# The mLSTM mixer of layer 1: scores and sums of values as three rounded passes on split operands, and the o gate kept in the place of y

## The chip, the cores and the metric

One core of a Trainium2 chip runs the whole program. The metric is the device time of one execution in microseconds. The kernel before took 2152.68 us (median of three runs, 2150.7 to 2155.58).

PE is the matmul engine (TensorE), PEld its weight loads, DVE the vector engine, ACT the scalar engine, POOL GpSimd, SP the engine that issues most DMAs. Each engine works through its instructions in order and waits on semaphores for the others.

## The reference

A backbone of four layers over 256 latent tokens and 256 context tokens of width 2048. Layer 1 is a bidirectional mLSTM with 8 heads (128 wide for q and k, 256 wide for v). The part that matters here, for one chunk of one direction:

```python
q, k, v, o, g, z = jnp.split(h @ w_in, idx, axis=-1)
...
s = jnp.einsum('bhtd,bhsd->bhts', q, k) * jnp.exp(dmat - m_t[..., None])
num = a[..., None] * jnp.einsum('bhtd,bhde->bhte', q, C) + jnp.einsum('bhts,bhse->bhte', s, v)
h = num / jnp.maximum(jnp.abs(den), jnp.exp(-m_t))[..., None]
...
y = jax.nn.sigmoid(o.astype(f32)).reshape(B, T, M_HEADS, M_DV) * h
y = _rmsnorm(y, hn.reshape(M_HEADS, M_DV)).reshape(B, T, M_V).astype(z.dtype)
return (y * jax.nn.silu(z)) @ w_out
```

The forward and backward directions are added. All is float32.

## The kernel before

All 512 tokens are worked on together, context first. Every big projection is a `gemm` (line 240): 16 contraction blocks of 128, four PSUM banks, and three rounded passes for each product. The weights are cast to `wh` (rounded, float32r) on ACT (L256), the remainder `wl` is taken on DVE (L257), the activations stand as `h` and `l` in the same way, and L298 adds `h*wh + h*wl + l*wh`. One such projection has 192 passes of 512 columns. `wh` and `wl` have three buffers each, the raw weights four.

Layer 1 has four pairs of heads. For each pair four projections run after each other: q and k (`done_qk`), v (`done_v`), o (`done_o`), z (`done_z`). Each has its `done` function called for each of its four banks, as soon as that bank is complete; the next projection takes the same four banks again (`psA`), so it waits for whatever `done` reads from them.

Between the projection's matmuls the mixer's own work of the pair is woven in, by a hand-written order of PE: a generator `core` is moved on by a step each time enough credit has come together (`fill.give`, a rate for each step of the projection; `CORE1` is the rate for the core during the o and z projections). One step of the projection is six matmuls. The core goes over eight tiles (two heads, four blocks of 128 queries each), each in three stages:

- `stage_a`: scores, one full-precision matmul of q against 256 keys (blocks 0 and 1, context) or 512 keys (blocks 2 and 3) into a bank `xb` (L803); the decay factors on ACT (`ef`, `eb`); products, row sums and the normalisation on DVE (L817 to L832). The result is `big`.
- `stage_b`: `big` is transposed on PE (L839) and copied to `wt` by ACT (L841).
- `stage_c`: the sums of values, full-precision matmuls of `wt` against `v` over two or four key blocks, 256 columns each (L848), then the o gate.

The four banks of `psX` (`xb`) go round among these. PE's order is written out by hand; for DVE, ACT and the other engines a scheduler orders the instructions when the program is built.

The o gate of `tanh` of o's projection is one tile `to` of 128 x 4 x 512. Tiles whose sums are ready before o is complete are copied to `yp` (L852) and gated later; the others are gated from the bank (L906). L908 then squares for the norm, into a scrap tile `jk`. `finish` (called `fin` in the weave) normalises, transposes on PE (L889), multiplies with hn and the z gate `zs` (L890) and stores the result to DRAM (L934), or splits it for the last pair.

In the background, other layers' modulation vectors are computed on DVE (`ada_dve`, L217): multiply and sum over 128 x 1024 tiles that come by DMA, moved on at the rates `BR1`. Below they are called multiplies. They stand in DVE's queue among all the rest.

The gates of all heads (`gates`) are computed once, during pair 0's v projection, in two scratch tiles, `sa` in the place of `yp` and `sb` in the place of `zs`.

Of the kernel before, what the change touches and what calls it, by code (L numbers as in the profile page):

```python
# [23 lines left out]

DV0 = (2, 4, 6)

NPE1, CORE1, ATT = 4, 0.4, 1.2
MIX3, MIX0, MIX1, FR0, BR0, AR0 = 0.55, 0.9, 0.7, 0.8, 0.34, 0.17

BR1 = ((0, 0.35, 0.25, 0.25), (0.35, 0.35, 0.25, 0.25), (0.4, 0.4, 0.3, 0.3), (0.5, 0.5, 0.35, 0.35))  # L30
# [21 lines left out]
def _build(tc, nc, top, A, out):  # L52
    V, S, G, T, Q = nc.vector, nc.scalar, nc.gpsimd, nc.tensor, nc.sync
# [644 lines left out]
    with ExitStack() as st:  # L698
        p1 = pool(st, "l1", reuse_waits="tile")

        def w2(name):
            return p1.tile([P, 512], F32, tag="w2", name=name, bufs=5)

        bgate = p1.tile([P, 1], F32, name="bgate")
        Q.dma_start(bgate, A["bgate"])
# [3 lines left out]
        def gates():  # L709


            gw = wp.tile([P, 2, 512], F32, tag="raw", name="gw", bufs=WRAW)
            Q.dma_start(gw[:, 0, :], A["w1gate"])
            Q.dma_start(gw[:, 1, :128], A["gsum"])

            pq = bank()
            for k4 in range(4):
                for ip in range(2):
                    for q in range(4):
                        kt = 4 * k4 + q  # L720
                        T.matmul(pq[32 * q:32 * q + 32, :], gw[:, 0, 32 * kt:32 * kt + 32], hl[kt][ip].bitcast(F32),
                                 start=k4 + ip == 0, stop=k4 == 3 and ip == 1)
                yield
            sq = w2("gq")
            S.copy(sq, pq)
            yield
            yield
            pg = bank()
            T.matmul(pg, gw[:, 1, :128], sq, start=True, stop=True)
            sa = pY.tile([P, 4, 512], F32, tag="yp", name="sa", bufs=1)  # L730
            sb = pY.tile([P, 4, 512], F32, tag="zs", name="sb", bufs=1)
            ri, rl, rb, rM, z0 = sa[:, 0, :], sa[:, 1, :], sa[:, 2, :], sa[:, 3, :], sb[:, 0, :]
# [25 lines left out]
            for n, src in enumerate((ri, rM, rb)):  # L758
                r = sb[:, n + 1, :]
# [21 lines left out]
        def core(c):  # L781
# [16 lines left out]
            def stage_a(hh, i, ub, um):  # L798
# [4 lines left out]
                T.matmul(sp[:, :ns], c.qk[:, hh, dg], c.qk[:, 2 + hh, :ns], start=True, stop=True)  # L803
# [31 lines left out]
            def stage_b(hh, i, big):  # L835
                ns = 256 if i < 2 else 512
                pt = bank()
                for k in range(ns // 128):
                    T.transpose(pt[:, 128 * k:128 * k + 128], big[:, 128 * k:128 * k + 128], ident)  # L839
                wt = p1.tile([P, 512], F32, tag="wt", name="wt", bufs=2)  # L840
                S.copy(wt[:, :ns], pt[:, :ns])  # L841
                return wt

            def stage_c(hh, i, wt):
                nb = 2 if i < 2 else 4
                po = bank()
                for k in range(nb):
                    T.matmul(po[:, :256], wt[:, 128 * k:128 * k + 128], c.v[:, k, 256 * hh:256 * hh + 256],  # L848
                             start=k == 0, stop=k == nb - 1)
                ys = c.yp[:, i, 256 * hh:256 * hh + 256]  # L850
                if c.pend is not None:
                    S.copy(ys, po[:, :256])  # L852
                    c.pend.append((hh, i))
                else:
                    c.gate(hh, i, po[:, :256])

            tiles = [(hh, i) for hh in range(2) for i in range(4)]
            u = {0: load(0)}
            w = {0: stage_a(0, 0, *u[0])}
            yield  # L860
            for n, (hh, i) in enumerate(tiles):
                if n == 2:
                    u[1] = load(1)
                if n + 1 < 8:
                    h2, i2 = tiles[n + 1]
                    w[n + 1] = stage_a(h2, i2, *u[h2])
                    yield
                if n:
                    stage_c(*tiles[n - 1], wt)
                    yield  # L870
                wt = stage_b(hh, i, w[n])
                yield
            yield
            stage_c(*tiles[-1], wt)
            yield

        def finish(c, sink):
            S.activation(c.ssq, c.ssq, AF.Sqrt, bias=eps4, scale=1.0 / 256)
# [16 lines left out]
        def make_pair(p):  # L895
            c = Pair()
            c.p = p
            c.qk = p1.tile([P, 4, 512], F32, tag="qk", name="qk", bufs=1)
            c.v = p1.tile([P, 4, 512], F32, tag="v", name="v", bufs=1)
            c.to = p1.tile([P, 4, 512], F32, tag="to", name="to", bufs=1)  # L900
            c.ssq = pY.tile([P, 8], F32, tag="ssq", name="ssq", bufs=2)
            c.pend = []

            def gate(hh, i, src):
                ys = c.yp[:, i, 256 * hh:256 * hh + 256]
                V.scalar_tensor_tensor(ys, c.to[:, i, 256 * hh:256 * hh + 256], 1.0, src, ALU.add, ALU.mult)  # L906
                jk = p1.tile([P, 256], F32, tag="jk", name="jk", bufs=1)
                S.activation(jk, ys, AF.Square, accum_out=c.ssq[:, 4 * hh + i:4 * hh + i + 1])  # L908

            c.gate = gate  # L910

            def done_qk(b, ps):
                S.activation(c.qk[:, b, :], ps, AF.Copy, scale=128 ** -0.5 if b < 2 else 1.0)

            def done_v(b, ps):
                S.copy(c.v[:, b, :], ps)

            def done_o(b, ps):
                S.activation(c.to[:, b, :], ps, AF.Tanh, scale=0.5)
                if b == 3:  # L920
                    pend, c.pend = c.pend, None
                    for hh, i in pend:
                        gate(hh, i, c.yp[:, i, 256 * hh:256 * hh + 256])

            def done_z(b, ps):
                tz = w2("tz")
                S.activation(tz, ps, AF.Tanh, scale=0.5)
                V.scalar_tensor_tensor(c.zs[:, b, :], tz, 1.0, ps, ALU.add, ALU.mult)

            c.done = (done_qk, done_v, done_o, done_z)  # L930
            return c

# [17 lines left out]
        for p in range(4):  # L950
# [9 lines left out]
            c.zs = pY.tile([P, 4, 512], F32, tag="zs", name="zs", bufs=1)  # L960
# [410 lines left out]
```

## Time and profile before

| | |
|---|---|
| median of three runs | 2152.68 us |
| the profiled execution | 2155.34 us, of which 2153.5 us are its span |
| granted TensorE clock, mean | 0.987 |
| HBM traffic | 435.9 MB read, 13.7 MB written |

In the 40 slices of the page each is 53.8 us, and layer 1 lies in slices 11 to 24:

```
PE   6899999999999999999999999999999999999998
DVE  4867888856787787799666678765645665567666
ACT  4332242223333324232332343223336544545444
PEclk7999999999999999999999999999999999999999
```

Each digit is the busy share in tenths. A row of the profile's groups gives line, engine, operation, tiles and shapes, then busy time, mean duration of one, and the idle time of that engine just before the group with what ended it. A float32 matmul stands as two records. Durations of matmuls overlap; the distance of two starts tells what one costs.

### The profile page before, as it was taken

To read this page: it belongs to the slowest core of one execution; us is meant where nothing else is said; L and a number is where in the kernel's file an instruction comes from. 1 tells how busy PE (TensorE), PEld (TensorE's weight loads), DVE (VectorE), ACT (ScalarE), POOL (GpSimd) and SP (SyncE) were. 2 spreads that over 40 slices of the span, in tenths; PEclk is the share of its full clock that TensorE was granted. 3 is DMA by queue.
4 is the path that set the end of the run, shared out by engine and by line. 5 is a ranking of instruction groups with operands and counts; after the bars stand their busy time and mean duration, and the time that the engine had idled before them with its cause. 6 is when DMAs were issued, how large, how long until landed. Compare 5 with 4: busy or idle time off the path is not lost. (4 is left out here: it accounts for less than half of the span.)

```text
span 2153.5 us, 29391 instructions
## 1 busy us (share of the span) xinstructions
PE 2091.3 (97%) x11190; PEld 1725.9 (80%) x11190; DVE 1527.3 (71%) x2793; ACT 812.2 (38%) x1338; POOL 19.3 (1%) x29
## 2 busy tenths in 40 slices
PE   6899999999999999999999999999999999999998
PEld 2668777788788888888888888888787777999986
DVE  4867888856787787799666678765645665567666
ACT  4332242223333324232332343223336544545444
POOL 0000000000000000000000000000000000000000
PEclk7999999999999999999999999999999999999999
DMA  9775778872465565477668667983243454564464
GB/s 349 275 265 191 250 276 282 322 271 95 153 209 166 199 224 179 162 250 254 202 207 305 226 235 280 335 312 107 88 137 124 141 176 138 173 195 138 153 194 147
DMA packets 126127, 451.52 MB, mean 210 GB/s; under 512 B 14224, under 2 KB 16784, under 8 KB 123296
## 3 DMA queue, kind: packets, MB, share of 16 engines
q1 hardware_dynamic: 125696, 448.71, 61.0%
q8 instruction: 88, 1.44, 0.3%
q10 hardware_dynamic: 288, 0.92, 0.1%
q14 instruction: 55, 0.45, 0.1%
HBM read 435.91 MB, written 13.66 MB: 209 GB/s over the span
## 5 line engine op out<-in xcount | busy, mean ns | idle before, releaser
L257 DVE TENSOR_TENSOR wl<-wraw,wh 128x1024 fp32r<-128x1024 f32 x400 | 489.1, 1224 | 404.6 <-ACT wh L256 393.4
L298 PE MATMUL acc<-h,wh 128*128 128x512 f32 (+1 forms) x1936 | 689.3, 356 | 6.1 <-ACT h L395 3.9
L256 ACT CAST wh<-wraw 128x1024 fp32r<-128x1024 f32 x400 | 419.1, 1049 | 724.4 <-PE acc L298 581.4
L298 PE MATMUL acc<-l,wh 128*128 128x512 f32 (+1 forms) x1936 | 671.7, 347 | 3.0 <-DVE l L396 1.8
L298 PE MATMUL acc<-h,wl 128*128 128x512 f32 (+1 forms) x1936 | 670.4, 346 | 1.3 <-DVE wl L257 1.1
L298 PE MATMUL acc<-wh,h 128*128 128x512 f32 x1024 | 427.0, 417 | 3.5 <-DVE xn L1019 2.2
L298 PEld LDWEIGHTS acc<-h,wh 128*128 128x128 f32 x1936 | 367.8, 190 | 61.9 <-issue 11.2
L298 PEld LDWEIGHTS acc<-l,wh 128*128 128x128 f32 x1936 | 367.3, 190 | 51.2 <-DVE l L396 3.5
L298 PEld LDWEIGHTS acc<-h,wl 128*128 128x128 f32 x1936 | 367.9, 190 | 45.7 <-DVE wl L257 2.3
L298 PE MATMUL acc<-wh,l 128*128 128x512 f32 x1024 | 401.2, 392 | 0.5 <-DVE l L396 0.5
L298 PE MATMUL acc<-wl,h 128*128 128x512 f32 x1024 | 399.7, 390 | 0.0
L217 DVE SCALAR_TENSOR_TENSOR araw<-araw,cb 128x1024 f32<-128x1024 f32 x300 | 364.7, 1223 | 12.0 <-DMA araw<-in_ada_t_dram 9.8
L298 PEld LDWEIGHTS acc<-wh,h 128*128 128x128 f32 x1024 | 192.8, 188 | 52.0 <-issue 14.5
L298 PEld LDWEIGHTS acc<-wl,h 128*128 128x128 f32 x1024 | 193.0, 188 | 44.6 <-issue 8.4
L298 PEld LDWEIGHTS acc<-wh,l 128*128 128x128 f32 x1024 | 192.5, 188 | 42.8 <-DVE l L396 1.3
L217 DVE SCALAR_TENSOR_TENSOR ajunk<-araw,cb 128x1024 f32<-128x1024 f32 x172 | 209.8, 1220 | 0.0
L187 PE MATMUL xb<-araw,cpad 128*32 128x256 f32 x672 | 56.7, 439 | 15.4 <-DMA araw<-in_ada_p_dram 12.7
L187 PEld LDWEIGHTS xb<-araw,cpad 128*32 128x32 f32 x672 | 17.6, 116 | 44.9 <-DMA araw<-in_ada_p_dram 26.9
L395 ACT ACTIVATE h<-mu,ada 128x256 fp32r<-128x256 f32 x80 | 36.9, 502 | 35.9 <-DVE mu L394 35.9
L848 PE MATMUL xb<-v,wt 128*128 128x256 f32 x192 | 46.7, 379 | 0.0
L453 ACT ACTIVATE sq<-rn 128x256 f32<-128x256 f32 (+1 forms) x48 | 24.7, 515 | 56.1 <-DVE rn L447 54.3
L908 ACT ACTIVATE jk<-yp 128x256 f32<-128x256 f32 x32 | 13.3, 417 | 78.8 <-DVE yp L906 78.8
(223 smaller groups left out, 1480.3 us busy)
## 6 DMA issues: line engine op xcount, KB each, us to landing
araw<-in_ada_t_dram SPq DMA_DIRECT2D x300, 512.0 KB, 5.2
wraw<-in_w1in_dram SPq DMA_DIRECT2D x128, 512.0 KB, 4.4
araw<-in_ada_p_dram SPq DMA_DIRECT2D x84, 512.0 KB, 5.4
wraw<-in_w2in_dram SPq DMA_DIRECT2D x80, 512.0 KB, 3.5
wraw<-in_w0g_dram SPq DMA_DIRECT2D x32, 512.0 KB, 5.5
wraw<-in_w0o_dram SPq DMA_DIRECT2D x32, 512.0 KB, 5.7
wraw<-in_w1o_dram SPq DMA_DIRECT2D x32, 512.0 KB, 7.0
wraw<-in_w2o_dram SPq DMA_DIRECT2D x32, 512.0 KB, 4.2
```

What stands on the lines that cost most here:

```text
L187: T.matmul(ps[32 * q:32 * q + 32, :256], cpad[:, 4 * kq + q, :], rv[:, q, :], start=kq == 0, stop=kq == 3)
L217: V.scalar_tensor_tensor(o, rv, 1.0, cb[:, v + 2 - nv, part], ALU.mult, ALU.mult, accum_out=am[:, v, i, hf:hf + 1])
L256: S.copy(wh, raw)
L257: pace.append(V.tensor_tensor(wl, raw, wh.bitcast(F32), ALU.subtract).ins)
L298: T.matmul(o, lhsT, rhs, start=start, stop=stop)
L395: S.activation(h[:, c], u, AF.Identity, bias=ada[:, l, SH, s, kt:kt + 1])
L453: S.activation(sq[:, c], rn[:, b, c], AF.Square)
L848: T.matmul(po[:, :256], wt[:, 128 * k:128 * k + 128], c.v[:, k, 256 * hh:256 * hh + 256], start=k == 0, stop=k == nb - 1)
L908: S.activation(jk, ys, AF.Square, accum_out=c.ssq[:, 4 * hh + i:4 * hh + i + 1])
```

## The change

Scores and sums of values become three passes of float32r operands, in the way of the projections.

- `c.qk` and `c.v` are now rounded (float32r). `done_qk` and `done_v` also write the remainders `ql` and `vl` on DVE, from the PSUM bank. `stage_b` rounds `wt` and writes its remainder `wtl` on DVE.
- L804: scores as `q*k + q*kl + ql*k`. L852: sums as `wt*v + wt*vl + wtl*v`.
- The tile `to` is no longer held: `done_o` writes `tanh` into `yp`, where the result will come (L937), or, where a tile's sum already stands there, into a small tile of 256 columns (L934), and gates it at once. The squares go into the PSUM bank that was just read; `jk` is gone.
- `ql` takes the place of `zs` in `pY` while the core runs. So `fin` of the pair before must be through when the first bank of q arrives, and the core must be through when the first bank of z arrives.
- `sb` becomes four tiles `w2`, which has six buffers rather than five.
- The core's order: two tiles' scores ahead, then for each tile b, the scores of the tile after next, c. `CORE1` goes from 0.4 to 0.56.

```diff
-NPE1, CORE1, ATT = 4, 0.4, 1.2
+NPE1, CORE1, ATT = 4, 0.56, 1.2
...
-            return p1.tile([P, 512], F32, tag="w2", name=name, bufs=5)
+            return p1.tile([P, 512], F32, tag="w2", name=name, bufs=6)
...
-            sb = pY.tile([P, 4, 512], F32, tag="zs", name="sb", bufs=1)
+            sb = [w2(f"sb{n}") for n in range(4)]
...
-                T.matmul(sp[:, :ns], c.qk[:, hh, dg], c.qk[:, 2 + hh, :ns], start=True, stop=True)
+                for ip, (q, k) in enumerate(((c.qk, c.qk), (c.qk, c.ql), (c.ql, c.qk))):
+                    T.matmul(sp[:, :ns], q[:, hh, dg], k[:, 2 + hh, :ns], start=ip == 0, stop=ip == 2)
...
-                wt = p1.tile([P, 512], F32, tag="wt", name="wt", bufs=2)
+                wt = p1.tile([P, 512], F32R, tag="wt", name="wt", bufs=2)
+                wtl = p1.tile([P, 512], F32R, tag="wtl", name="wtl", bufs=2)
                 S.copy(wt[:, :ns], pt[:, :ns])
-                return wt
+                V.tensor_tensor(wtl[:, :ns], pt[:, :ns], wt[:, :ns].bitcast(F32), ALU.subtract)
+                return wt, wtl
...
                 for k in range(nb):
-                    T.matmul(po[:, :256], wt[:, 128 * k:128 * k + 128], c.v[:, k, 256 * hh:256 * hh + 256],
-                             start=k == 0, stop=k == nb - 1)
+                    for ip, (w, v) in enumerate(((wt[0], c.v), (wt[0], c.vl), (wt[1], c.v))):
+                        T.matmul(po[:, :256], w[:, 128 * k:128 * k + 128], v[:, k, 256 * hh:256 * hh + 256],
+                                 start=k + ip == 0, stop=k == nb - 1 and ip == 2)
                 ys = c.yp[:, i, 256 * hh:256 * hh + 256]
-                if c.pend is not None:
+                if (hh, i) in c.to:
+                    c.gate(hh, i, ys, po[:, :256])
+                else:
                     S.copy(ys, po[:, :256])
-                    c.pend.append((hh, i))
-                else:
-                    c.gate(hh, i, po[:, :256])
+                    c.po.add((hh, i))
...
             for n, (hh, i) in enumerate(tiles):
-                if n == 2:
+                if n == 1:
                     u[1] = load(1)
-                if n + 1 < 8:
-                    h2, i2 = tiles[n + 1]
-                    w[n + 1] = stage_a(h2, i2, *u[h2])
-                    yield
-                if n:
-                    stage_c(*tiles[n - 1], wt)
-                    yield
-                wt = stage_b(hh, i, w[n])
+                wt = stage_b(hh, i, w.pop(n))
                 yield
-            yield
-            stage_c(*tiles[-1], wt)
-            yield
+                if n + 2 < 8:
+                    h2, i2 = tiles[n + 2]
+                    w[n + 2] = stage_a(h2, i2, *u[h2])
+                yield
+                stage_c(hh, i, wt)
+                yield
...
-            def gate(hh, i, src):
+            def gate(hh, i, to, src, junk=None):
                 ys = c.yp[:, i, 256 * hh:256 * hh + 256]
-                V.scalar_tensor_tensor(ys, c.to[:, i, 256 * hh:256 * hh + 256], 1.0, src, ALU.add, ALU.mult)
-                jk = p1.tile([P, 256], F32, tag="jk", name="jk", bufs=1)
-                S.activation(jk, ys, AF.Square, accum_out=c.ssq[:, 4 * hh + i:4 * hh + i + 1])
+                V.scalar_tensor_tensor(ys, to, 1.0, src, ALU.add, ALU.mult)
+                S.activation(src if junk is None else junk, ys, AF.Square, accum_out=c.ssq[:, 4 * hh + i:4 * hh + i + 1])
...
             def done_qk(b, ps):
-                S.activation(c.qk[:, b, :], ps, AF.Copy, scale=128 ** -0.5 if b < 2 else 1.0)
+                if b == 0:
+
+                    fill.finish(f"fin{p - 1}")
+                    c.ql = pY.tile([P, 4, 512], F32R, tag="zs", name="ql", bufs=1)
+                sc = 128 ** -0.5 if b < 2 else 1.0
+                S.activation(c.qk[:, b, :], ps, AF.Copy, scale=sc)
+                V.scalar_tensor_tensor(c.ql[:, b, :], ps, sc, c.qk[:, b, :].bitcast(F32), ALU.mult, ALU.subtract)

             def done_v(b, ps):
                 S.copy(c.v[:, b, :], ps)
+                V.tensor_tensor(c.vl[:, b, :], ps, c.v[:, b, :].bitcast(F32), ALU.subtract)

             def done_o(b, ps):
-                S.activation(c.to[:, b, :], ps, AF.Tanh, scale=0.5)
-                if b == 3:
-                    pend, c.pend = c.pend, None
-                    for hh, i in pend:
-                        gate(hh, i, c.yp[:, i, 256 * hh:256 * hh + 256])
+                for hh in range(2):
+                    cols = slice(256 * hh, 256 * hh + 256)
+                    ys = c.yp[:, b, cols]
+                    if (hh, b) in c.po:
+                        to = p1.tile([P, 256], F32, tag="to", name="to", bufs=1)
+                        S.activation(to, ps[:, cols], AF.Tanh, scale=0.5)
+                        gate(hh, b, to, ys, ps[:, cols])
+                    else:
+                        S.activation(ys, ps[:, cols], AF.Tanh, scale=0.5)
+                        c.to.add((hh, b))

             def done_z(b, ps):
+                if b == 0:
+                    fill.finish(f"core{p}")
+                    c.zs = pY.tile([P, 4, 512], F32, tag="zs", name="zs", bufs=1)
                 tz = w2("tz")
```

How this moves instructions is shown at three places, by rows of the two built programs (line, operation, what is written and read, shape).

First PE in pair 0, at a tile with four key blocks. Before, a tile's transposes (L839), the scores of a later tile (L803) and the sums (L848) stand apart, with passes of the projection between them; here the sums with the passes on either side:

```order
L298 MATMUL acc<-wl,h_4712 128x512
L298 MATMUL acc<-wh,l_4713 128x512
L848 MATMUL xb<-v,wt 128x256 x4
L298 MATMUL acc<-wh,h_4682 128x512
L298 MATMUL acc<-wl,h_4682 128x512
L298 MATMUL acc<-wh,l_4683 128x512
```

The change has, for a tile of four blocks of the same pair, twelve instructions there, each group of three ending with the one that reads `wtl`:

```order
L298 MATMUL acc<-wh,l_4637 128x512
L852 MATMUL xb<-v,wt 128x256
L852 MATMUL xb<-vl,wt 128x256
L852 MATMUL xb<-v,wtl 128x256
L852 MATMUL xb<-v,wt 128x256
L852 MATMUL xb<-vl,wt 128x256
L852 MATMUL xb<-v,wtl 128x256
```

Six of the twelve are shown; the same three follow twice more. A score is one instruction before and three now.

Second DVE in pair 0, at the scores of its last tile (128x512). Before, the remaining steps of that tile follow with little between, and the next two gates:

```order
L817 SCALAR_TENSOR_TENSOR ef,dn<-xb,ef 128x512
L819 SCALAR_TENSOR_TENSOR eb,dn<-xb,eb 128x512
L257 TENSOR_TENSOR wl<-wraw,wh 128x1024
L822 SCALAR_TENSOR_TENSOR da<-dn 128x2
L823 TENSOR_TENSOR da<-da,em 128x2
L824 RECIPROCAL da<-da 128x2
L831 TENSOR_SCALAR ef<-ef,da 128x512
L832 SCALAR_TENSOR_TENSOR ef<-eb,da,ef 128x512
L906 SCALAR_TENSOR_TENSOR yp<-to,xb 128x256
```

In the change, behind the first product of that tile (L818, 128x512), up to the remainder `wtl` of the tile before it:

```order
L820 SCALAR_TENSOR_TENSOR eb,dn<-xb,eb 128x512
L217 SCALAR_TENSOR_TENSOR araw,am<-araw,cb 128x1024
L823 SCALAR_TENSOR_TENSOR da<-dn 128x2
L257 TENSOR_TENSOR wl<-wraw,wh 128x1024
L824 TENSOR_TENSOR da<-da,em 128x2
L910 SCALAR_TENSOR_TENSOR yp<-yp,xb 128x256
L825 RECIPROCAL da<-da 128x2
L217 SCALAR_TENSOR_TENSOR ajunk,am<-araw,cb 128x1024
L832 TENSOR_SCALAR ef<-ef,da 128x512
L217 SCALAR_TENSOR_TENSOR araw,am<-araw,cb 128x1024
L833 SCALAR_TENSOR_TENSOR ef<-eb,da,ef 128x512
L844 TENSOR_TENSOR wtl<-xb,wt 128x512
```

Three multiplies of the background now stand among this tile's steps, and `wtl` (L844), which PE needs, stands behind them. On PE, from the scores of the last tile to the third pass of the sums of the tile before it, there are 40 passes of the projection, the sums of a tile with two blocks, four transposes and two passes.

Third ACT at the last bank of pair 0's o projection. Before, one tanh over the whole bank (the L919 row; the rows around it serve the tiles and the weights):

```order
L256 CAST wh<-wraw 128x1024
L813 ACTIVATE eb<-ub_5424,negM 128x128
L919 ACTIVATE to<-acc 128x512
L256 CAST wh<-wraw 128x1024
L908 ACTIVATE jk,ssq<-yp 128x256
```

In the change, at the same bank: for its first half a tanh (L934), a square into the bank (L911, which needs the gate on DVE between), and then the tanh of the other half (L937):

```order
L934 ACTIVATE to<-acc 128x256
L256 CAST wh<-wraw 128x1024
L911 ACTIVATE acc,ssq<-yp 128x256
L937 ACTIVATE yp<-acc 128x256
L911 ACTIVATE xb,ssq<-yp 128x256
L843 CAST wt<-xb 128x256
```

The bank is free only after the last of its three reads and writes, where before it was free after one.

More of the change, by code (lines that the diff above doesn't have):

```diff
@@ L730, in gates @@
             sa = pY.tile([P, 4, 512], F32, tag="yp", name="sa", bufs=1)
-            sb = pY.tile([P, 4, 512], F32, tag="zs", name="sb", bufs=1)
-            ri, rl, rb, rM, z0 = sa[:, 0, :], sa[:, 1, :], sa[:, 2, :], sa[:, 3, :], sb[:, 0, :]
+            sb = [w2(f"sb{n}") for n in range(4)]
+            ri, rl, rb, rM, z0 = sa[:, 0, :], sa[:, 1, :], sa[:, 2, :], sa[:, 3, :], sb[0]
             S.activation(ri[0:64, :], pg[0:64, :], AF.Identity, bias=bgate[0:64])
@@ L758, in gates @@
             for n, src in enumerate((ri, rM, rb)):
-                r = sb[:, n + 1, :]
+                r = sb[n + 1]
                 V.tensor_copy(r[0:32, :], src[0:32, :])
@@ L847, in stage_c @@
                 for k in range(nb):
-                    T.matmul(po[:, :256], wt[:, 128 * k:128 * k + 128], c.v[:, k, 256 * hh:256 * hh + 256],
-                             start=k == 0, stop=k == nb - 1)
+                    for ip, (w, v) in enumerate(((wt[0], c.v), (wt[0], c.vl), (wt[1], c.v))):
+                        T.matmul(po[:, :256], w[:, 128 * k:128 * k + 128], v[:, k, 256 * hh:256 * hh + 256],
+                                 start=k + ip == 0, stop=k == nb - 1 and ip == 2)
                 ys = c.yp[:, i, 256 * hh:256 * hh + 256]
-                if c.pend is not None:
+                if (hh, i) in c.to:
+                    c.gate(hh, i, ys, po[:, :256])
+                else:
                     S.copy(ys, po[:, :256])
-                    c.pend.append((hh, i))
-                else:
-                    c.gate(hh, i, po[:, :256])
+                    c.po.add((hh, i))
             tiles = [(hh, i) for hh in range(2) for i in range(4)]
             u = {0: load(0)}
-            w = {0: stage_a(0, 0, *u[0])}
+            w = {}
+            for n in range(2):
+                w[n] = stage_a(*tiles[n], *u[0])
+                yield
             yield
             for n, (hh, i) in enumerate(tiles):
-                if n == 2:
+                if n == 1:
                     u[1] = load(1)
-                if n + 1 < 8:
-                    h2, i2 = tiles[n + 1]
-                    w[n + 1] = stage_a(h2, i2, *u[h2])
-                    yield
-                if n:
-                    stage_c(*tiles[n - 1], wt)
-                    yield
-                wt = stage_b(hh, i, w[n])
-                yield
-            yield
-            stage_c(*tiles[-1], wt)
-            yield
+                wt = stage_b(hh, i, w.pop(n))
+                yield
+                if n + 2 < 8:
[3 more added lines that the diff above has]
+                stage_c(hh, i, wt)
+                yield
         def finish(c, sink):
@@ L897, in make_pair @@
             c.p = p
-            c.qk = p1.tile([P, 4, 512], F32, tag="qk", name="qk", bufs=1)
-            c.v = p1.tile([P, 4, 512], F32, tag="v", name="v", bufs=1)
-            c.to = p1.tile([P, 4, 512], F32, tag="to", name="to", bufs=1)
+            c.qk = p1.tile([P, 4, 512], F32R, tag="qk", name="qk", bufs=1)
+            c.v = p1.tile([P, 4, 512], F32R, tag="v", name="v", bufs=1)
+            c.vl = p1.tile([P, 4, 512], F32R, tag="vl", name="vl", bufs=1)
             c.ssq = pY.tile([P, 8], F32, tag="ssq", name="ssq", bufs=2)
-            c.pend = []
@@ L904, in gate @@
-            def gate(hh, i, src):
+            c.to, c.po = set(), set()
+            def gate(hh, i, to, src, junk=None):
                 ys = c.yp[:, i, 256 * hh:256 * hh + 256]
-                V.scalar_tensor_tensor(ys, c.to[:, i, 256 * hh:256 * hh + 256], 1.0, src, ALU.add, ALU.mult)
-                jk = p1.tile([P, 256], F32, tag="jk", name="jk", bufs=1)
-                S.activation(jk, ys, AF.Square, accum_out=c.ssq[:, 4 * hh + i:4 * hh + i + 1])
+                V.scalar_tensor_tensor(ys, to, 1.0, src, ALU.add, ALU.mult)
+                S.activation(src if junk is None else junk, ys, AF.Square, accum_out=c.ssq[:, 4 * hh + i:4 * hh + i + 1])
@@ L959, in _build @@
                 fill.finish(f"fin{p - 1}")
-            c.zs = pY.tile([P, 4, 512], F32, tag="zs", name="zs", bufs=1)
             c.yp = pY.tile([P, 4, 512], F32, tag="yp", name="yp", bufs=1)
```

## The prediction

> **What bounds the kernel now.** I read the page first, then the stretch in which layer 1 runs (about 560 to 1330 us), by stretches and by groups.
>
> ```profile
> span 2153.5 us, 29391 instructions
> PE 2091.3 (97%) x11190; PEld 1725.9 (80%) x11190; DVE 1527.3 (71%) x2793; ACT 812.2 (38%) x1338; POOL 19.3 (1%) x29
> ```
>
> ```profile
> 560.00:1330.00 770.00, 770.00 (x3475) 626.08 (x3474) 596.50 (x1138) 265.35 (x452) 19.08 (x25) 1.00 0.66 220
> 920.00:964.00 44.00, 44.00 (x204) 36.45 (x203) 40.95 (x68) 13.27 (x21) 0.00 (x0) 1.00 0.77 255
> 964.00:1007.00 43.00, 43.00 (x192) 35.59 (x191) 39.45 (x64) 10.69 (x12) 0.00 (x0) 1.00 0.76 253
> ```
>
> After the stretch and its length come the busy times of PE, PEld, DVE, ACT and POOL, then the granted clock. In layer 1 PE is busy 770.00 of 770 us at clock 1.00; DVE 596.50, ACT 265.35. A busy PE row proves little, since ends are modelled, so I looked at what PE waited for there:
>
> ```profile
> L298 PE MATMUL acc<-wh,h 128*128 128x512 f32 x512 | 209.8, 410 | 0.0
> ...
> L298 PE MATMUL acc<-h,wl 128*128 128x512 f32 x483 | 188.2, 390 | 0.0
> L848 PE MATMUL xb<-v,wt 128*128 128x256 f32 x192 | 46.7, 379 | 0.0
> L803 PE MATMUL xb<-qk 128*128 128x512 f32 x32 | 16.4, 592 | 0.0
> ```
>
> The last column is idle time ahead of a group: 0.0 in these, so neither the weight stream nor the mixer's chain is ever late there. Matmul time removed in layer 1 shortens the run one for one, as long as nothing else becomes late. That is the whole question: how much matmul time goes, and whether DVE, which gets the splitting, keeps up.
>
> **What goes from PE.** Durations of matmuls are latencies, so I price a group by starts: from the last L298 ahead of it to the second L298 behind it, less two ordinary steps of L298.
>
> ```profile
> 618.23 0.40 PE L298 MATMUL acc<-wh,l 128*128 128x512 f32 x1
> 618.46 0.60 PE L803 MATMUL xb<-qk 128*128 128x256 f32 x2
> 618.71 0.58 PE L298 MATMUL acc<-wh,h 128*128 128x512 f32 x1
> 619.13 0.40 PE L298 MATMUL acc<-wl,h 128*128 128x512 f32 x1
> ```
>
> ```profile
> 641.86 0.40 PE L298 MATMUL acc<-wh,l 128*128 128x512 f32 x1
> 642.09 1.02 PE L803 MATMUL xb<-qk 128*128 128x512 f32 x2
> ...
> 643.19 0.40 PE L298 MATMUL acc<-wl,h 128*128 128x512 f32 x1
> ...
> 645.47 0.40 PE L298 MATMUL acc<-wh,l 128*128 128x512 f32 x1
> 645.70 1.03 PE L848 MATMUL xb<-v,wt 128*128 128x256 f32 x4
> ...
> 646.79 0.40 PE L298 MATMUL acc<-wl,h 128*128 128x512 f32 x1
> ```
>
> ```profile
> 703.96 0.40 PE L298 MATMUL acc<-l,wh 128*128 128x512 f32 x1
> 704.19 1.89 PE L848 MATMUL xb<-v,wt 128*128 128x256 f32 x8
> ...
> 706.15 0.39 PE L298 MATMUL acc<-h,wl 128*128 128x512 f32 x1
> ```
>
> One step of L298 (a rounded pass, 512 columns): ten starts from 643.19 to 645.47, so 0.228 us. A full-precision score over 256 keys: 0.90 - 0.456 = 0.444 us; over 512 keys: 1.33 - 0.456 = 0.874. Sums of values over two key blocks: 1.32 - 0.456 = 0.864; over four: 2.19 - 0.456 = 1.734. A full-precision product stands as two records.
>
> A rounded pass with 256 columns does not occur in layer 1, but it does where the chain of waits runs through layer 2's output projection:
>
> ```profile
> 1847.10 85.69 PE acc L298 x714
> ```
>
> That is 0.120 us each, every one with its own weight load. So three passes cost 0.360 (256 keys), 0.684 (512 keys), 0.720 (two blocks) and 1.440 (four blocks). Each pair has four tiles of the small and four of the large kind, and there are four pairs, so each difference counts 16 times: 16 x (0.084 + 0.190 + 0.144 + 0.294) = **11.4 us less**. Unknown is how such passes run in short groups between 512-wide ones: half the 512-wide step, 0.114, would give 2.0 us more (336 passes of 256 columns), 0.144 each would leave them without gain. I take 0.120, the measured row.
>
> **What comes to DVE and ACT.**
>
> ```profile
> L217 DVE SCALAR_TENSOR_TENSOR araw<-araw,cb 128x1024 f32<-128x1024 f32 x176 | 214.5, 1226 | 5.8 <-DMA araw<-in_ada_t_dram 4.1
> L257 DVE TENSOR_TENSOR wl<-wraw,wh 128x1024 fp32r<-128x1024 f32 x125 | 153.4, 1227 | 126.4 <-ACT wh L256 119.8 <-DMA araw<-in_ada_t_dram 5.4 <-DMA wraw<-in_w1in_dram 1.0
> ...
> L890 DVE SCALAR_TENSOR_TENSOR zs<-xb,hn,zs 128x512 f32<-128x512 f32 x16 | 11.9, 745 | 0.0
> ...
> L906 DVE SCALAR_TENSOR_TENSOR yp<-to,xb 128x256 f32<-128x256 f32 x20 | 8.2, 412 | 14.0 <-PE xb L848 14.0
> L947 DVE TENSOR_TENSOR l<-l,h 128x512 fp32r<-128x512 f32 x12 | 8.1, 689 | 4.6 <-ACT h L946 4.4
> ```
>
> ```profile
> L256 ACT CAST wh<-wraw 128x1024 fp32r<-128x1024 f32 x126 | 132.2, 1050 | 260.9 <-PE acc L298 195.8 <-issue 30.5 <-DMA wraw<-in_w1in_dram 11.9
> L908 ACT ACTIVATE jk<-yp 128x256 f32<-128x256 f32 x32 | 13.3, 417 | 78.8 <-DVE yp L906 78.8
> ...
> L919 ACT ACTIVATE to<-acc 128x512 f32<-128x512 f32 x16 | 9.5, 593 | 15.2 <-PE acc L298 15.2
> ...
> L841 ACT COPY wt<-xb 128x512 f32<-128x512 f32 x16 | 9.3, 584 | 16.7 <-PE xb L839 16.7
> ```
>
> Remainders, priced by the nearest rows: `ql` 16 x 0.745 = 11.9, `vl` 16 x 0.689 = 11.0, `wtl` 16 x 0.689 + 16 x 0.412 = 17.6; together 40.5 us. DVE in layer 1 goes from 596.5 to 637 of some 760 us, 84%. On ACT, 32 tanh of 256 columns (by L908 at most 0.417 each, 13.3 us) replace 16 of 512 (9.5): 3.8 us on an engine with 500 idle. As totals both fit. What counts is four places where PE could wait.
>
> *The remainder of the weights (`wtl`).* Before, PE's sums of values needed only ACT's copy (0.584). Now their third pass needs DVE as well, whose queue is in order. The rows shown above for pair 0 are the tightest I found: between the scores of tile 7 and the third pass of tile 6, DVE has (L818 and L820 0.69 each, multiplies 1.23 three times, the split of weights 1.23, three small ones 0.16 each, gate 0.41, L832 0.55, L833 0.75, `wtl` 0.69) about 9.2 us; PE has 40 steps of L298, 9.1, sums 0.72, transposes 0.44 and two passes 0.24, in all 10.5. Cover: 1.3 us, less any lateness DVE has there already. Bounds: nothing (below it there is nothing to win, PE has no idle here), or one multiply, 1.23 us, for each of the 20 tiles (five a pair) that fall into the o projections, where DVE gets fullest, 25 us. The place above lies just behind one. Most tiles have more cover than this one, so I stay near the row of zero waits and take **2 us** lost over all.
>
> *Banks of the projections.* `ql` and `vl` hold a PSUM bank until DVE has read it. The next projection touches its fourth bank 18 steps after the last matmul, 4.1 us. Copy 0.6, two multiplies ahead 2.45, remainder 0.745: 3.8. It just fits; DVE's tightest stretch is pair 2, 920 to 1007, where 40.95 + 3.0 of 44 and 39.45 + 2.8 of 43 us are filled. Nothing counted; bound 1.2 us (a third multiply) at each of eight such boundaries, 10 us. Instructions that work like this are there already: L928 reads the z banks on DVE, and L298 shows no wait.
>
> *The o gate.* A bank now goes tanh, gate, square into the bank, tanh: 0.42 + 0.41 + 0.42 + 0.42, with a cast of 1.05 between, 2.7 us, against the same 4.1. Nothing. For a backlog behind it, the bound above stands.
>
> *`ql` in `zs`'s place.* It must wait until the last pair's `zs` has left for DRAM.
>
> ```profile
> 743.29 0.74 DVE L890 SCALAR_TENSOR_TENSOR zs<-xb,hn,zs 128x512 f32<-128x512 f32 x1
> ```
>
> ```profile
> 757.81 0.60 ACT L913 ACTIVATE qk<-acc 128x512 f32<-128x512 f32 x1 [1.67 <-PE acc L298]
> ```
>
> ```profile
> DMA to landing us min/median/max: 4.2/5.3/7.0
> ```
>
> Last product done at 744.0, landed by 751.1 at the latest, first needed at 758.4: 7 us of cover (the row is that of the store L934). If it went, DVE would stand, with splits of weights behind. The sixth buffer of `w2` and `sb`'s move cost nothing: `sb` is read out before the mixer starts.
>
> **Sum.** 11.4 - 2 = 9.4 us off. The profiled execution took 2155.3, so 2145.9 by its own time; it is the upper of the runs shown, 2.7 above their median 2152.7. On the median: **2143**.
>
> **Rivals.** *DVE becomes the bound in projections.* Bank waits take their 10 us: 2152.7 - 11.4 + 10 = 2151, no change. For it: 44 us filled in 44; against it: before, 40.95 in 44 made no wait. 10%.
>
> *`wtl` makes it slower.* If each of the 20 tiles in the o projections stands behind one more multiply pair than in my rows (2.45 - 1.3 = 1.15 us short), 23 us are lost: 2164. It decides from 15.7 us lost, 0.8 us per tile. For it: an in-order queue at 90%; against it: backlogs of that length would already delay L298's weights today. 6%.
>
> *Weight loads set the pace.* Three passes load three times where full precision loaded twice.
>
> ```profile
> L298 PEld LDWEIGHTS acc<-h,wl 128*128 128x128 f32 x1936 | 367.9, 190 | 45.7 <-DVE wl L257 2.3
> ```
>
> If loads of 0.19 us could not lie beside matmuls, 256-wide passes would take 0.19 each: 48 score passes and 288 value passes at 0.07 more than taken above, 23.5 us, so 2152.7 - 11.4 + 23.5 = 2165. The 714 passes at 0.120 speak against it: loads of 0.19 lie over each other and over the matmuls there. 2%.
>
> By the Trainium skill, "TensorE: Matmul & The Clock Gate" (Part 3, What overlaps and what doesn't), a load overlaps matmuls in flight only where the row group differs, which full-height passes never do, so it stands for this rival (its Part 2 also lets a load go ahead into a background buffer). The trace disagrees with the first, with 0.120 per pass against 0.190 per load.
>
> *The passes bring more* (0.114 and no waits): 13.4 off, 2139. 4%.
>
> My forecast keeps 78%. The range goes from 2139 less half the spread of the runs, 2137, to a loss of 9 us, 2150. About 0.2%, 4.3 us, is what a measurement of this kernel tells from no change: faster by more 0.82, within 0.10, slower 0.08.
>
> **What would show it.** Right: scores and sums of values gone from two records per product to three passes, with starts 0.120 (256 columns) and 0.228 (512) apart; PE still 0.0 idle ahead of L298 between 560 and 1320; layer 2 starting some 9 us earlier. Wrong on DVE: waits of PE for `wtl`, `ql`, `vl` or `wl`, first in the o projections and in pair 2's q and v. Wrong on the passes: starts of 0.144 or more. The forecast falls if PE's waits in layer 1 pass 7 us.

## The result and the profile after

The change takes 2145.33 us (median of five runs, 2138.84 to 2146.01), the kernel before 2155.58 us beside it (five runs, 2150.7 to 2159.31): 10.2 us less by the medians. The ratio taken over the runs is 0.9948, with a 95% interval of 0.9936 to 0.9961 (the quotient of the two medians is 0.9952). The profiled execution took 2144.03 us, against 2155.34 before.

The page's first lines of the change:

```profile
span 2142.2 us, 29748 instructions
## 1 busy us (share of the span) xinstructions
PE 2078.6 (97%) x11318; PEld 1724.8 (81%) x11318; DVE 1556.1 (73%) x2857; ACT 820.8 (38%) x1360; POOL 16.9 (1%) x29
```

PE is 12.7 us less busy, DVE 28.8 more. Two of the passages that were priced before, in the timeline of the change (start, duration, then line and shape): a score over 512 keys, then the sums of a tile with two key blocks.

```profile
630.25 0.40 PE L298 MATMUL acc<-wh,l 128*128 128x512 f32 x1
630.49 0.39 PE L804 MATMUL xb<-qk 128*128 128x512 f32 x1
630.71 0.40 PE L804 MATMUL xb<-ql,qk 128*128 128x512 f32 x1
630.95 0.39 PE L804 MATMUL xb<-qk,ql 128*128 128x512 f32 x1
631.18 0.39 PE L298 MATMUL acc<-wh,h 128*128 128x512 f32 x1
631.41 0.40 PE L298 MATMUL acc<-wl,h 128*128 128x512 f32 x1
```

```profile
633.68 0.40 PE L298 MATMUL acc<-wh,l 128*128 128x512 f32 x1
633.92 0.28 PE L852 MATMUL xb<-v,wt 128*128 128x256 f32 x1
...
634.51 0.28 PE L852 MATMUL xb<-v,wtl 128*128 128x256 f32 x1
634.63 0.39 PE L298 MATMUL acc<-wh,h 128*128 128x512 f32 x1
634.86 0.40 PE L298 MATMUL acc<-wl,h 128*128 128x512 f32 x1
```

From the last L298 ahead to the second behind, less two steps of 0.228: the score costs 1.16 - 0.456 = 0.70 us (0.874 before), the six passes of the sums 1.18 - 0.456 = 0.72 (0.864 before).

What PE waited for in layer 1 and its output projection, 555 to 1490 us of the change (total, times, longest):

```profile
PE xb L371 <- DVE sqacc L454: 1.1, 1, 1.1
PE acc L298 <- ACT h L395: 1.0, 1, 1.0
PE acc L298 <- DVE l L396: 0.5, 1, 0.5
PE xb L852 <- DVE wtl L844: 0.3, 1, 0.3
PE acc L298 <- DVE zs L946: 0.2, 1, 0.2
```

The first three belong to the norms at the layer's two ends, and before has them too (it also has one of 0.3 us for `wl` in the output projection). New are one wait for `wtl` and one for the last z bank, together 0.5 us, both in pair 3.

Whole times scatter by several us from run to run, so I measure the stretch in which only layer 1's work runs: from the first copy of a q bank to the last `rn` of its output projection. Both ends are starts that stand in the rows of the two lines (minimum, median and maximum in ns, then first and last start). Before:

```profile
L913 ACT ACTIVATE qk<-acc x16: 597/598/601, 552.4 to 1155.8; 128x512 f32<-128x512 f32 x16
```

```profile
L447 DVE SCALAR_TENSOR_TENSOR rn<-acc,ada,rold x32: 469/476/485, 1343.3 to 1486.2; 128x256 f32<-128x256 f32 x32
```

The change:

```profile
L921 ACT ACTIVATE qk<-acc x16: 597/599/601, 555.2 to 1150.0; 128x512 fp32r<-128x512 f32 x16
```

```profile
L447 DVE SCALAR_TENSOR_TENSOR rn<-acc,ada,rold x32: 472/477/486, 1335.5 to 1477.9; 128x256 f32<-128x256 f32 x32
```

933.8 us before (1486.2 - 552.4), 922.7 in the change (1477.9 - 555.2): **11.1 us** less. (Starts are printed to a tenth of a us; differences here are taken before rounding.) The rest of the 11.3 us between the spans of these two executions nearly cancels: layer 0 took 2.8 us longer (552.4 against 555.2), and two starts of layers behind layer 1 came out some 1.5 us shorter each, by the clock (last section).

### The profile page after: what moved, and what is told of

It is laid out like the page before. It is cut to its first block, busy times and chain, and to the rows that moved or that the text cites. A ratio compares the mean times of both kernels' runs of the same rounds, so it can differ in the third digit from the quotient of the medians.

```text
span 2142.2 us, 29748 instructions
## 1 busy us (share of the span) xinstructions
PE 2078.6 (97%) x11318; PEld 1724.8 (81%) x11318; DVE 1556.1 (73%) x2857; ACT 820.8 (38%) x1360; POOL 16.9 (1%) x29
## 5 line engine op out<-in xcount | busy, mean ns | idle before, releaser
L298 PE MATMUL acc<-h,wh 128*128 128x512 f32 (+1 forms) x1936 | 680.7, 352 | 6.3 <-ACT h L395 3.9
L298 PE MATMUL acc<-l,wh 128*128 128x512 f32 (+1 forms) x1936 | 670.8, 346 | 3.0 <-DVE l L396 1.8
L298 PE MATMUL acc<-h,wl 128*128 128x512 f32 (+1 forms) x1936 | 669.8, 346 | 1.0 <-DVE wl L257 0.9
L298 PE MATMUL acc<-wh,h 128*128 128x512 f32 x1024 | 419.4, 410 | 3.5 <-DVE xn L1036 2.2
L298 PEld LDWEIGHTS acc<-h,wh 128*128 128x128 f32 x1936 | 367.0, 190 | 60.3 <-issue 9.5
L298 PEld LDWEIGHTS acc<-l,wh 128*128 128x128 f32 x1936 | 366.7, 189 | 50.9 <-DVE l L396 3.5
L298 PEld LDWEIGHTS acc<-h,wl 128*128 128x128 f32 x1936 | 367.2, 190 | 43.1 <-DVE wl L257 1.7
L298 PE MATMUL acc<-wh,l 128*128 128x512 f32 x1024 | 400.8, 391 | 0.5 <-DVE l L396 0.5
L298 PE MATMUL acc<-wl,h 128*128 128x512 f32 x1024 | 399.3, 390 | 0.0
L298 PEld LDWEIGHTS acc<-wh,h 128*128 128x128 f32 x1024 | 192.7, 188 | 49.3 <-issue 12.6
L298 PEld LDWEIGHTS acc<-wh,l 128*128 128x128 f32 x1024 | 192.3, 188 | 42.6 <-DVE l L396 1.3
L298 PEld LDWEIGHTS acc<-wl,h 128*128 128x128 f32 x1024 | 192.8, 188 | 41.7 <-issue 6.5
L1073 DVE TENSOR_REDUCE mx<-xb 128x1 f32<-128x512 f32 x32 | 22.0, 688 | 26.5 <-PE xb L1071 26.3
L447 DVE SCALAR_TENSOR_TENSOR rn<-acc,ada,rold 128x256 f32<-128x256 f32 x80 | 35.9, 479 | 6.8 <-PE acc L298 6.6
```

The costliest lines, as they stand in the source:

```text
L298: T.matmul(o, lhsT, rhs, start=start, stop=stop)
L447: V.scalar_tensor_tensor(rn[:, b, a:a + 256], ps[:, 256 * s - o:256 * s - o + 256], ada[:, l, GA, s, kt:kt + 1], ro[:, b, a:a + 256], ALU. ...
L1073: V.tensor_reduce(mx, sp, AX.X, ALU.max, negate=True)
```

## Experiments

Each is one profiled execution of a kernel made from the change, and its stretch is read from the same two rows as above; 933.8 (before) and 922.7 (the change) are what to compare with. The granted clock is 1.00 throughout the stretch in all of them but two, where it is said. Two profiles of one and the same kernel (the last two experiments) give 921.73 and 921.72, so differences of a few tenths can be read.

**The scores alone.** `c.v`, `wt` in full precision, without `vl` and `wtl` (of this edit and the next ones only the main lines are shown):

```diff
-                    for ip, (w, v) in enumerate(((wt[0], c.v), (wt[0], c.vl), (wt[1], c.v))):
-                        T.matmul(po[:, :256], w[:, 128 * k:128 * k + 128], v[:, k, 256 * hh:256 * hh + 256],
-                                 start=k + ip == 0, stop=k == nb - 1 and ip == 2)
+                    T.matmul(po[:, :256], wt[0][:, 128 * k:128 * k + 128], c.v[:, k, 256 * hh:256 * hh + 256],
+                             start=k == 0, stop=k == nb - 1)
```

> Only the scores run as three passes (qk rounded, ql kept); the sums of values are full-precision matmuls again, without vl and wtl. All else, the order too, is that of the change. Measure: the stretch of layer 1 from the first copy of a q bank to the last rn of its output projection, 933.8 us before and 922.7 in the change. Theory (matmul time alone): 16 x (0.444 - 0.36) + 16 x (0.874 - 0.70) = 4.1 us less than before, so 929.7. Rival (DVE's new work costs time of its own): ql makes banks late, 930.5 or more, and PE waits for DVE show.

Measured 929.6 (556.4 to 1486.0), 4.2 less than before. The matmul theory holds to 0.1 us; PE's only wait for DVE inside the pairs is 0.4 us, for the last z product.

**The sums alone.** `c.qk` in full precision, without `ql`:

```diff
-                for ip, (q, k) in enumerate(((c.qk, c.qk), (c.qk, c.ql), (c.ql, c.qk))):
-                    T.matmul(sp[:, :ns], q[:, hh, dg], k[:, 2 + hh, :ns], start=ip == 0, stop=ip == 2)
+                T.matmul(sp[:, :ns], c.qk[:, hh, dg], c.qk[:, 2 + hh, :ns], start=True, stop=True)
```

> Only the sums of values run as three passes (vl and wtl kept); the scores are full-precision matmuls again, without ql. Theory: 16 x (0.864 - 0.72) + 16 x (1.734 - 1.44) = 7.0 us less than before, so a stretch of 926.8, with at most 1 us of waits for wtl. Rival (waits for wtl eat part of it): 928 or more, with PE waiting for L844 in several tiles of each pair.

Measured 926.7 (555.9 to 1482.6), 7.1 less than before, without a wait for `wtl`; PE waits 0.7 us for the last z product. The two parts nearly add up: 4.2 + 7.1 = 11.3, the whole 11.1. But both carry the new order, which has a price of its own.

**The order alone.** Both edits above at once: what is left is the new order, the o gate and the moved tiles.

> Full-precision scores and sums, no remainders, but the core's new order, CORE1 0.56, the o gate in y's place and sb in w2 as in the change. Theory: PE does the same matmuls as before and waits for nothing, 933.8, within 0.3. Rival (part of the gain is the order's or the gate's): clearly under 933.8; or the gate's longer hold of the banks costs: over 934.5 with PE waiting for L934, L937 or L911.

Measured 934.6 (555.1 to 1489.7), 0.8 more than before. PE waits, 555 to 1340 us:

```profile
PE acc L298 <- DVE zs L938: 1.1, 1, 1.1
PE acc L298 <- DVE l L396: 0.5, 1, 0.5
```

No gain comes from the order or from the gate, and no wait is for the gate's lines, so its longer hold of the banks costs nothing. But together they have a small price: 1.1 us at the end of pair 3, where PE waits for a z bank that DVE has yet to read. That is just over the 934.5 that I had given the rival, by another mechanism than the one named there. Counted from this run, the scores are worth 5.0 us, the sums 7.9 and both together 11.9: that the two parts met the whole so closely above is in part luck, since each of them carries the order's price and a z wait of another length. Without PE's waits (1.1 here, 0.4, 0.7, and 0.4 in the change) they are worth 4.3 and 7.4, and both together 11.2.

**No wait for `wtl`.** The third pass reads `wt` again (its product with the remainder is left out):

```diff
-                    for ip, (w, v) in enumerate(((wt[0], c.v), (wt[0], c.vl), (wt[1], c.v))):
+                    for ip, (w, v) in enumerate(((wt[0], c.v), (wt[0], c.vl), (wt[0], c.v))):
...
-                V.tensor_tensor(wtl[:, :ns], pt[:, :ns], wt[:, :ns].bitcast(F32), ALU.subtract)
```

> The third pass of the sums reads wt again in place of wtl, and wtl is not computed: same matmuls on PE, no wait for the remainder, 17.6 us less on DVE. The sums lack the product of wtl and v. Theory (the change loses under 1 us to DVE): a stretch of 922.2, that is 0.5 less than the change, no PE wait for DVE left in it. Rival (in-order DVE costs the 2 us that the prediction set aside, or more): 920.7 or less.

Measured 922.4 (555.1 to 1477.5), 0.2 under the change. So the remainder of the weights, 32 instructions on DVE and a third pass that needs it, costs 0.2 us net. I had expected no wait for DVE to be left; that for the z bank stays, with 0.6 us.

**A fourth pass.** `wtl` times `vl` added to the sums (`stop` moves to it):

```diff
-                    for ip, (w, v) in enumerate(((wt[0], c.v), (wt[0], c.vl), (wt[1], c.v))):
+                    for ip, (w, v) in enumerate(((wt[0], c.v), (wt[0], c.vl), (wt[1], c.v), (wt[1], c.vl))):
```

> The change with a fourth pass in the sums of values (wtl times vl), 96 x 2 more... counted by key blocks: 2 or 4 per tile, 96 more passes of 256 columns with their own weight loads. Theory (a pass costs its step of 0.120 us, loads lie beside): 96 x 0.120 = 11.5 us more, a stretch of layer 1 of 934.2. Rival (weight loads of 0.19 us set the pace): 18 us more, 940.7. Either way the gain of the values is given back, which shows the layer bound by PE one for one.

Measured 933.8 (553.0 to 1486.8), 11.2 more than the change for 96 passes: 0.116 us each. Weight loads, of 0.19 us each by the row of the prediction, do not set the pace, and PE's time goes into the stretch one for one.

**`wtl` computed three and five times over.** Each further subtraction writes the same tile again, so PE waits for the last:

```diff
-                V.tensor_tensor(wtl[:, :ns], pt[:, :ns], wt[:, :ns].bitcast(F32), ALU.subtract)
+                for _ in range(3):
+                    V.tensor_tensor(wtl[:, :ns], pt[:, :ns], wt[:, :ns].bitcast(F32), ALU.subtract)
```

> The change with each wtl computed three times over: 35 us more on DVE in layer 1, and wtl ready 0.8 us (256 keys) or 1.4 us (512 keys) later at the least. Nothing else differs. Theory (cover of 1.3 us at the tightest tile, more elsewhere; DVE at some 87%): PE waits for wtl in a few tiles, 1 to 6 us in all, a stretch of 924 to 929. Rival (the change just fits, an in-order DVE has no cover left): every tile pays what is added, 16 x 0.8 + 16 x 1.4 = 35 us, 958.

> The change with each wtl computed five times over: 70 us more on DVE in layer 1, wtl 1.7 or 2.8 us later at the least. Theory (cover between 1.3 and some 3 us by tile): most tiles of the o projections wait now, 0.5 to 1.5 us each, so 10 to 30 us, a stretch of 933 to 953, that is no gain left or a loss. Rival (DVE's idle time of some 120 us takes it): under 930.

Three times: 931.5 (554.2 to 1485.7), 8.8 more than the change. PE's waits in the pairs:

```profile
PE xb L853 <- DVE wtl L845: 8.0, 4, 2.8
PE acc L298 <- DVE zs L947: 0.4, 1, 0.4
```

Four tiles wait, 28 do not: there is cover, though I had the waits (1 to 6 us) and the stretch (924 to 929) too low. Five times: 994.0 (554.8 to 1548.8), 71 more, far over my 933 to 953.

```profile
PE xb L853 <- DVE wtl L845: 45.8, 18, 5.7
```

Waits explain 46 of the 71 us. DVE's rows at pair 0's first tile show why a short instruction comes so late:

```profile
630.24 0.41 DVE L845 TENSOR_TENSOR wtl<-xb,wt 128x256 fp32r<-128x256 f32 x1
630.93 0.56 DVE L818 SCALAR_TENSOR_TENSOR ef<-xb,ef 128x384 f32<-128x384 f32 x1 [0.28 <-PE xb L804]
...
632.76 1.22 DVE L217 SCALAR_TENSOR_TENSOR ajunk<-araw,cb 128x1024 f32<-128x1024 f32 x1
...
634.31 1.22 DVE L217 SCALAR_TENSOR_TENSOR araw<-araw,cb 128x1024 f32<-128x1024 f32 x1
635.45 0.08 DVE L217 DVE_READ_ACCUMULATOR araw<-araw,cb 128x1 f32 x1
635.45 0.42 DVE L845 TENSOR_TENSOR wtl<-xb,wt 128x256 fp32r<-128x256 f32 x1
```

Between the first and the fifth subtraction of 0.42 us each lie 5.2 us, since the scheduler set other work between them, two multiplies of 1.22 among it. And behind this wait PE runs slower. The rows of PE there:

```profile
635.92 0.39 PE L853 MATMUL xb<-v,wtl 128*128 128x256 f32 x1 [2.05 <-DVE wtl L845]
...
637.42 0.63 PE L298 MATMUL acc<-wh,l 128*128 128x512 f32 x1
637.84 0.63 PE L298 MATMUL acc<-wh,h 128*128 128x512 f32 x1
```

and the same stretch by windows (PE, PEld, DVE, ACT, POOL busy, granted clock, DMA):

```profile
636.40:639.80 3.40, 3.40 (x11) 2.72 (x10) 3.40 (x6) 0.77 (x2) 0.00 (x0) 0.50 0.79 222
```

Steps of L298 are 0.42 us there rather than 0.228, at a granted clock of 0.50: a wait of 2.05 us was paid once as idle time and once more as 3.4 us at half speed, 1.7 us. Over 560 to 1400 us the granted clock is 0.97 on average:

```profile
560.00:1400.00 840.00, 794.21 (x3653) 652.26 (x3652) 687.98 (x1339) 276.51 (x475) 15.45 (x25) 0.97 0.61 205
```

That is 840 x 0.03 = 25 us by estimate, and with the 46 us of waits it makes up the 71.

**The same load on DVE, where nobody waits for it.** The change with four subtractions per tile into a scrap tile, placed behind `wtl` (they read `cb` rather than a PSUM bank):

```diff
                 V.tensor_tensor(wtl[:, :ns], pt[:, :ns], wt[:, :ns].bitcast(F32), ALU.subtract)
+                for _ in range(4):
+                    jk = ap_.tile([P, 1024], F32, tag="junk", name="djunk", bufs=1)
+                    V.tensor_tensor(jk[:, :ns], cb[:, 0, :ns], cb[:, 1, :ns], ALU.subtract)
```

> The change with the same 70.5 us more on DVE as in the run with five wtl, but as four subtractions per tile into a scrap tile that nobody waits for, placed behind wtl. The stretch there was 994.0, 71 over the change. Theory (what costs is the time by which wtl comes late, not DVE's total): most of it vanishes, under 950, with PE waits of 5 to 25 us. Rival (DVE as a whole is the bound once its slack is used): again some 990.

Measured 927.5 (555.1 to 1482.6), 4.8 more than the change, against 71. Equal instructions by count and size on an engine that is then busy 684 of 770 us, where the change has 627:

```profile
560.00:1330.00 770.00, 766.51 (x3628) 632.14 (x3627) 683.97 (x1331) 274.66 (x474) 17.05 (x25) 1.00 0.65 221
```

PE's waits in the pairs are under the 5 to 25 us that I had expected:

```profile
PE acc L298 <- DVE wl L257: 2.0, 1, 2.0
PE acc L298 <- DVE zs L949: 1.2, 1, 1.2
PE xb L855 <- DVE wtl L844: 0.3, 1, 0.3
```

The 2.0 us are one late split of weights, and the clock falls behind it:

```profile
684.00:692.00 8.00, 6.05 (x21) 4.63 (x20) 8.00 (x12) 1.44 (x2) 0.00 (x0) 0.79 0.39 136
```

8 x 0.21 = 1.7 us by estimate; with the waits (3.5, of which the change has 0.4) that is the 4.8. So it is the place in the queue ahead of a result that PE wants, not DVE's total, that costs.

**Fewer multiplies in pair 3's z projection.**

```diff
-BR1 = ((0, 0.35, 0.25, 0.25), (0.35, 0.35, 0.25, 0.25), (0.4, 0.4, 0.3, 0.3), (0.5, 0.5, 0.35, 0.35))
+BR1 = ((0, 0.35, 0.25, 0.25), (0.35, 0.35, 0.25, 0.25), (0.4, 0.4, 0.3, 0.3), (0.5, 0.5, 0.35, 0.2))
```

> The change with the background's rate in pair 3's z projection 0.2 rather than 0.35: five or so steps of one or two multiplies fewer there, done later. Theory (the only PE waits left, for wtl and for the last z product of pair 3, come from multiplies ahead of them in DVE's queue): pair 3 loses its wait, a stretch of 922.0 to 922.3. Rival (the wait is from the y tiles loaded and split in that projection): unchanged, 922.7.

Measured 921.7 (556.2 to 1477.9), 0.9 less than the change and 0.3 under the range that I gave. No PE wait is left in the pairs. That fits the theory for the z bank, but the wait for `wtl` went another way. Ahead of `wtl` DVE has L965, the split of a y tile, in both kernels; in the change DVE stood idle for it, since ACT's `h` (L964) waited for the tile's load. ACT's row in the change, then in this run:

```profile
1272.52 1.29 ACT L964 CAST h<-l 128x512 fp32r<-128x512 f32 x2 [2.62 <-DMA l<-ytd]
```

```profile
1270.65 1.14 ACT L964 CAST h<-l 128x512 fp32r<-128x512 f32 x2
```

In the change the loads of two y tiles were issued from 1266.9 us on, 0.4 us behind a background load of 512 KB, and ACT started on them 5.6 us later; here they were issued from 1267.6 on, without that load just ahead, and ACT started 3.0 us later. So this wait came from the y tiles, as the rival said, and by these rows the background held it up through its load, not through a multiply in DVE's queue; no run separates the two. This is the shortest stretch of all, and was timed:

> The change with the background's rate in pair 3's z projection 0.2 rather than 0.35, timed against the kernel before. By its profile, layer 1 is 0.9 us shorter than in the change and 12.1 shorter than before. Theory: 12 us faster than before in the median, ratio 0.9944, not to be told from the change's 0.9948. Rival (work moved out of the projection comes back later): 0.996 or more.

2145.16 us (five runs, 2142.46 to 2146.3), before 2156.24 (nine runs, 2151.8 to 2157.24): ratio 0.9947, interval 0.9933 to 0.996. Its profile gives the same 921.7 again. It beats the kernel before; the change's 0.9948 can't be told from it.

## Why the prediction was right

- *PE bounds layer 1 one for one.* Shown both ways: 4.2 and 7.1 us less for the two parts, 11.2 more for 96 passes added.
- *The prices of passes.* 0.70 and 0.72 us stand against 0.684 and 0.720 in the sum, and the parts measured, 4.2 and 7.1 (4.3 and 7.4 without waits), against 4.4 and 7.0 there. The row of layer 2 (0.120 us per pass of 256 columns) carried over; 0.116 was measured here.
- *DVE's load.* Of the 40.5 us worked out, 28.8 show as busy time. Durations of neighbours lie over each other, which is at least part of it: in pair 2's q projection below each `ql` lasts 0.69 us and the next instruction starts 0.60 after it.
- *2 us lost to waits for `wtl`.* Too much, and at the wrong place. Without `wtl` only 0.2 us come back; all loss to DVE that a small edit could remove is 0.9 us. The place that I had called the tightest, pair 0's tile 6, made no wait: there `wtl` is through at 686.8 us and the third pass starts at 688.65, a cover of 1.9 us where I had 1.3. What waited was pair 3, where L965 (the split of y for the output projection, waiting for ACT's `h`) stands ahead of `wtl`:

```profile
1273.17 1.37 DVE L965 TENSOR_TENSOR l<-l,h 128x512 fp32r<-128x512 f32 x2 [1.88 <-ACT h L964]
1274.45 0.68 DVE L844 TENSOR_TENSOR wtl<-xb,wt 128x512 fp32r<-128x512 f32 x1
```

```profile
1274.65 0.28 PE L852 MATMUL xb<-vl,wt 128*128 128x256 f32 x1
1275.19 0.39 PE L852 MATMUL xb<-v,wtl 128*128 128x256 f32 x1 [0.26 <-DVE wtl L844]
```

  I had looked at multiplies ahead of `wtl`, not at work of the next stage that itself waits (here for a load).
- *Banks.* Counted at nothing, and in three pairs they cost nothing. Pair 2's q banks on DVE:

```profile
952.21 1.22 DVE L217 SCALAR_TENSOR_TENSOR ajunk<-araw,cb 128x1024 f32<-128x1024 f32 x1
953.36 0.08 DVE L217 DVE_READ_ACCUMULATOR ajunk<-araw,cb 128x1 f32 x1
953.36 0.69 DVE L922 SCALAR_TENSOR_TENSOR ql<-acc,qk 128x512 fp32r<-128x512 f32 x1
953.96 1.22 DVE L217 SCALAR_TENSOR_TENSOR araw<-araw,cb 128x1024 f32<-128x1024 f32 x1
...
959.13 0.69 DVE L922 SCALAR_TENSOR_TENSOR ql<-acc,qk 128x512 fp32r<-128x512 f32 x1
```

  One remainder and two multiplies per bank, without a gap, 2.9 us where PE completes a bank every 2.7. So DVE falls behind there, but the fourth ends at 959.8, some 2 us before PE wants the bank (the next projection starts at 957.8 and touches it 18 steps later), where I had worked out 0.3. The z bank of pair 3, which I had taken as safe because its kind made no wait before, did wait (0.2 us, and 1.1 with the order alone).
- *The o gate and `ql` in `zs`'s place.* Nothing, as said: no PE wait names them.
- *The rivals.* Weight loads as the pace: the fourth pass excludes it. DVE as the bound: four subtractions more per tile beside the path cost 4.8 us, with DVE busy 57 us longer. `wtl` making it slower: the mechanism exists, but of the two loads tried, 70 us more work ahead of `wtl` turns the gain into a loss, and 35 us more still leaves 2.3 of 11.1 us.

The sum was 9.4 us, the medians show 10.2 and the stretch 11.1; the difference between the first and the last is mostly the 2 us set aside. That the medians come within 0.8 us of the sum is in part luck: too large a loss for `wtl` stands against the scatter of whole times. (2143 was counted from 2152.7; beside the change the kernel before took 2155.58, so it is the differences that compare.)

## What to carry to other kernels

Where PE has no idle time in a stage, a full-precision matmul turned into three rounded passes gives its difference one for one, and the difference can be read from rows of rounded passes elsewhere in the trace. What has to be checked is not the total of the engine that makes the remainders, but what stands ahead of each remainder in its queue, work of the next stage and the loads that this work waits for included. The same DVE work cost 71 us ahead of what PE waited for and 5 us behind it.

## What the hardware showed unexpectedly

A wait of some 2 us on PE may cost more than itself, by chance. The profile of before has a clock of 0.81 in the 6 us at the start of layer 2, the change 1.00 at the same place, where in both PE waits 2.2 us for DVE (L1019 and L1036). The windows of before and then of the change:

```profile
1538.00:1544.00 6.00, 3.83 (x13) 2.79 (x12) 4.81 (x10) 1.34 (x2) 0.00 (x0) 0.81 0.38 115
```

```profile
1530.00:1536.00 6.00, 3.83 (x20) 3.01 (x19) 5.18 (x9) 1.46 (x3) 0.00 (x0) 1.00 0.34 98
```

PE is busy for 3.83 us in both, with 13 matmuls in the one and 20 in the other. That is the 1.5 us seen there, with as much again at the start of layer 3 (0.83 over 10 us before, 1.00 in the change): part of why whole runs scatter by several us while the stretch of layer 1 can be compared to a few tenths. Nor did every wait have this price: with `wtl` computed three times PE waited four times for it, up to 2.8 us, and the clock stayed at 1.00:

```profile
560.00:1330.00 770.00, 761.54 (x3611) 627.92 (x3610) 652.75 (x1265) 273.88 (x474) 18.16 (x25) 1.00 0.65 220
```

The Trainium skill, "TensorE: Matmul & The Clock Gate" (Part 1), says that the clock is set by the activity in windows of about 3.4 us that run freely, which agrees with the 3.4 us at half clock above. That waits of 2.05 and 2.2 us, shorter than a window, can be enough is what this case's traces show.
